# Sums of squares of the memory queries: squares as the weights of 32-column tiles with one column of ones, instead of ones as weights and a masked sum; and layer one's twelve transposes held four groups of matmuls longer

## The chip, the cores and the metric

One Trainium2 chip, one core of it. The metric is device microseconds (us) of one execution of the whole kernel, the median of three runs. The engines are named as the profile names them: PE is TensorE's matmuls, PEld its weight loads, DVE is VectorE, ACT is ScalarE, POOL is GpSimd, SP is SyncE, whose queue issues the loads of the weights.

## What is computed

Two layers of a hybrid decoder trunk over 256 tokens of width 1024. What matters here is one of three branches, attention of the tokens to a memory, with its query norm, and beside it the block-sparse attention whose probabilities are transposed (with 256 tokens its only block is the causal one).

```python
for l in range(2):
    h = rms_norm(x, norm_g[l])
    q_a, k_a, v_a, q_h, f_h, i_h, q_m, z = split(h @ w_in[l])          # eight groups of columns
    o_a = causal_attention(rope(rms_norm(q_a)), rope(rms_norm(k_a)), v_a)   # 8 heads x 64
    o_h = rms_norm(hgrn2(q_h, f_h, i_h))                               # 4 heads x 128
    qm  = rms_norm(q_m.reshape(B, S, 4, 128), mem_q_norm[l])           # a sum of 128 squares per token and head
    o_m = softmax(qm @ km.T / sqrt(128)) @ vm                          # km, vm from the 256 memory tokens
    x = x + (concat(o_a, o_h, o_m) * silu(z)) @ w_out[l]
```

## The kernel before

**Work and stages.** Every large product is made three times with float32 split into a high and a low part (`wh`, `wl` of the weights, `hT` or `yh`, `yl` of the other side), and added up in PSUM. The weights come in chunks of 128x1024: SP loads one into a buffer `wr`, ACT makes the high part of it (`h_to`, line 143), DVE the low part (`l_to`, line 158), PE uses both. There are four `wh` and three `wl` buffers, so ACT and DVE can be a few chunks ahead of PE and no more. A layer goes through its groups of columns in a fixed order, among them the query of the memory branch (`group_a` with `g_qm`, lines 263 and 1145) and right behind it the value of block-sparse attention (`group_b` with `g_va`, lines 204 and 729), and ends with the product with `w_out` (`w_out_phase`, line 1250; its matmuls are on line 1265). A `group_a` has four heads of one chunk each, every head eight groups of three matmuls of 256 columns (lines 272 to 274: `wh` twice, then `wl`). A `group_b` has four chunks of twelve matmuls of 512 columns (lines 213 to 216).

**What sets the order.** All else (norms, softmax, transposes) is written as generators that `step` (line 170) advances a piece at a time, at slots in the matmul loops; `yield n` waits n slots, `room` waits for one of four PSUM tiles named `sd`. Where the code doesn't pin instructions, the framework's scheduler orders them when the program is built. The order of each engine is then fixed: an instruction that waits holds all that stands behind it on its engine.

**Around the change.** `g_qm` is called with the accumulators of two heads at a time. ACT casts them to `qmh` (line 1153) and squares them into `sq` (line 1155): 128 partitions are the 128 numbers of a head, the columns are (head of the pair, half of the tokens t, group g of 32 tokens, token s). The sums over the partitions are wanted with tokens on the partitions. Before, eight matmuls a layer (line 1165, recorded at the helper's line 202 with tiles `sd` and `sq,ones`) take 32 columns of ones as weights and 128 columns of squares as the moving side; each puts into 32 partitions 32 equal rows. DVE then multiplies with a repeated identity `m32` (line 1168) and adds up (line 1170), which leaves each token its own sum in `ssq`; `rsq` (line 595) makes of it the inverse root, on DVE (line 597) and POOL. The scores of the memory branch (line 1193) don't need it; their softmax does (lines 1202 and 1208).

**The transposes.** `g_moba_unit(l, u)` (line 1040) is the softmax of half of the eight block-sparse heads: exponentials on ACT (line 1086), their sums' reciprocal `ria` on DVE (line 1091), eight multiplications of `P` by it on DVE (line 1095: four of 128x128 for the first half of the tokens, then four of 128x256), and twelve transposes on PE (line 1108) in three blocks of four, each block into one `sd` tile that ACT copies out (line 1109). For u = 1 the first block needs only the first four multiplications. For u = 0 in layer one, line 1099 holds the transposes until head 2 of the memory query is done, and line 1107 has the scheduler put them behind the matmul `T["last"]`. PSUM tiles that they may wait for are those of `y_transpose` (line 777; PE line 781, ACT line 784, DVE line 785).

Of the kernel before, what the change touches and what calls it, by code (L numbers as in the profile page):

```python
# [12 lines left out]
F32 = mybir.dt.float32  # L13
# [5 lines left out]
OP = mybir.AluOpType  # L19
AX = mybir.AxisListType  # L20
# [26 lines left out]
def hymba_kernel(ctx: ExitStack, tc: tile.TileContext, front, x, x_t, mem, mem_t, positions, w_in, w_out, w_mem_kv,  # L47
                 moba_g, out):
    nc = tc.nc
    cst = ctx.enter_context(tc.tile_pool(name="cst", bufs=1))  # L50
    sb = ctx.enter_context(tc.tile_pool(name="sb", bufs=1))
# [6 lines left out]
    def acc_tile():  # L58
        return psum.tile([128, 512], F32, name="acc", tag="acc", bufs=4)
# [4 lines left out]
    def room(what, n=1):  # L64
        while held[what] + n > room_of[what]:
            yield

    def take(*whats):
        for w in whats:
            yield from room(w)  # L70
        while any(held[w] >= room_of[w] for w in whats):
            yield
        for w in whats:
            held[w] += 1

    def side_tile():
        held["sd"] += 1
        assert held["sd"] <= 4
        return psum.tile([128, 512], F32, name="sd", tag="sd", bufs=4)

    def rel(what="sd", n=1):
        held[what] -= n

    def small(name, n):
        return sb.tile([128, n], F32, name=name, tag=name, bufs=2)
# [39 lines left out]
    def dma_to(n):  # L125
        while st["dma"] < min(n, len(chunks)):
            i = st["dma"]
            ap = chunks[i][1]
            raws[i] = sb.tile([128, 1024], F32, name="wr", tag="wr", bufs=RAW_BUFS)
            load(raws[i], ap)  # L130
            st["dma"] += 1
# [4 lines left out]
    def h_to(n):  # L136
        while st["h"] < min(n, len(chunks)):
            i = st["h"]
            off = 16 if chunks[i][0] == "A" else 0
            whs[i] = sb.tile([128, 1088], F32R, name="wh", tag="wh", bufs=WH_BUFS)[:, off:off + 1024]  # L140
            g = chunks[i][2]
            if g is None:
                ins = nc.scalar.copy(whs[i], raws[i])  # L143
                if i == 12:
                    pin(ins)
            else:
                for sl in parts(i):
                    nc.scalar.activation(whs[i][:, sl], raws[i][:, sl], AF.Copy, scale=gT[:, g:g + 1])  # L148
            st["h"] += 1

    def l_to(n):
        while st["l"] < min(n, len(chunks)):
            i = st["l"]
            off = 16 if chunks[i][0] == "A" else 0
            wls[i] = sb.tile([128, 1088], F32R, name="wl", tag="wl", bufs=WL_BUFS)[:, off:off + 1024]
            g = chunks[i][2]
            if g is None:
                nc.vector.tensor_tensor(wls[i], raws[i], whs[i].bitcast(F32), op=OP.subtract)  # L158
            else:
                for sl in parts(i):  # L160
                    nc.vector.scalar_tensor_tensor(wls[i][:, sl], in0=raws[i][:, sl], scalar=gT[:, g:g + 1],  # L161
                                                   in1=whs[i][:, sl].bitcast(F32),
                                                   op0=OP.mult, op1=OP.subtract)
            st["l"] += 1

    active = []
    done = set()
    T = {}

    def step():  # L170
        for e in list(active):
            e[0] -= 1
            if e[0] <= 0:
                try:
                    e[0] = next(e[1]) or 1
                except StopIteration:
                    active.remove(e)

    def spawn(gen, delay=1):
        active.append([delay, gen])  # L180
# [8 lines left out]
    def slot(first):  # L189
        if first:  # L190
            c = st["c"]
            dma_to(c + 1 + DMA_AHEAD)
            h_to(c + 1 + H_AHEAD)
            l_to(c + 1 + L_AHEAD)
        step()

    def mm(o, a, b, s, e):
        nc.tensor.matmul(o, lhsT=a, rhs=b, start=s, stop=e)  # L198


    def mm_row(o, a, b):
        tc.keep_in_program_order(nc.tensor.matmul(o, lhsT=a, rhs=b, start=True, stop=True))  # L202
# [60 lines left out]
    def group_a(thl, each, name=None):  # L263

        for h in range(4):
            i = st["c"]
            if h % 2 == 0:
                acc = acc_tile()
            o = acc[:, (h % 2) * 256:(h % 2) * 256 + 256]
            for k in range(8):  # L270
                wH, wL = whs[i][:, k * 128:(k + 1) * 128], wls[i][:, k * 128:(k + 1) * 128]
                mm(o, wH, thl[:, k, 0], k == 0, False)
                mm(o, wH, thl[:, k, 1], False, False)
                last = nc.tensor.matmul(o, lhsT=wL, rhs=thl[:, k, 0], start=False, stop=k == 7)  # L274
                if k == 3:
                    slot(False)
            T["last"] = last.ins
            done.add((name, h))
            st["c"] += 1
            del whs[i], wls[i], raws[i]  # L280
            if h % 2:
                spawn(each(h - 1, acc))
            slot(True)
# [45 lines left out]
    pt = side_tile()  # L329
# [3 lines left out]
    ident = cst.tile([128, 128], F32, name="ident")  # L333
# [253 lines left out]
    def heads(t, n):  # L587
        return t.rearrange("p (h d) -> p h d", h=n)
# [6 lines left out]
    def rsq(name, ss, n, width):  # L595
        ms = small(name + "m", n)
        nc.vector.tensor_scalar(ms, ss, 1.0 / width, EPS, op0=OP.mult, op1=OP.add)
        r = small(name + "r", n)
        nc.gpsimd.tensor_tensor(r, ms, pw[:, :n], op=OP.pow)
        return r  # L600
# [55 lines left out]
        T["vm"] = vmh, vml  # L656
        yield

    m32 = cst.tile([128, 32], F32, name="m32")
    ones32 = cst.tile([128, 32], F32, name="ones32")  # L660

    def g_m32():
        nc.vector.memset(ones32, 1.0)
        nc.vector.tensor_reduce(m32, ident.rearrange("p (g s) -> p s g", g=4), AX.X, OP.add)
        yield

    lbs = cst.tile([128, 2, 4], F32, name="lbs")

# [371 lines left out]
    def g_moba_unit(l, u):  # L1040
# [10 lines left out]
        for t in range(2):  # L1051
# [18 lines left out]
            for i in range(4):  # L1070
                c = t * 4 + i
# [11 lines left out]
        for t in range(2):  # L1083
            for i in range(4):
                c, r = t * 4 + i, t * 8 + 2 * i + u
# [6 lines left out]
        for t in range(2):  # L1092
            for i in range(4):
                c = t * 4 + i
                nc.vector.tensor_scalar(P[:, i, kc[t]], P[:, i, kc[t]], ri[:, c:c + 1], None, op0=OP.mult)  # L1095
        yield 2
        tag = ("PTh", "PTl")[u]
        yield from take(tag)
        while u == l == 0 and ("qm0", 2) not in done:
            yield  # L1100
        PT = sb.tile([128, 4, 384], F32, name="PT", tag=tag, bufs=1)
        for b in (1, 2, 0) if u == 0 and l == 1 else range(3):
            bs = slice(b * 128, (b + 1) * 128)
            yield from room("sd")
            pt = side_tile()
# [17 lines left out]
        for w in range(2):  # L1123
            for i in range(4):
                p, e = 2 * w + i // 2, i % 2
                h = 2 * p + e
                rows, c = slice(64 * e, 64 * e + 64), (i // 2) * 256
# [17 lines left out]
    def g_qm(l, h0, acc):  # L1145
        if h0 == 0:
            T["qm"] = (sb.tile([128, 4, 256], F32R, name="qmh", tag="ih", bufs=1),
                       sb.tile([128, 1088], F32R, name="qml", tag="hF", bufs=1)[:, 16:1040].rearrange(
                           "p (k s) -> p k s", k=4))
            T["q2"] = []  # L1150
        qmh, qml = T["qm"]
        hs, a = slice(h0, h0 + 2), heads(acc, 2)
        nc.scalar.copy(qmh[:, hs], a)
        sq = sb.tile([128, 512], F32, name="sq", tag="sq", bufs=2)
        nc.scalar.activation(sq, acc, AF.Square)
        T["q2"].append(sq.rearrange("p (h t g s) -> p h t g s", h=2, t=2, g=4))
        nc.vector.tensor_tensor(qml[:, hs], a, qmh[:, hs].bitcast(F32), op=OP.subtract)
        if h0 == 0:
            return
        yield 2  # L1160
        yield from room("sd")
        pt = side_tile()
        for u, sq in reversed(list(enumerate(T.pop("q2")))):
            for g in range(4):
                mm_row(pt[g * 32:g * 32 + 32, u * 128:u * 128 + 128], ones32, sq[:, :, :, g])
        ss = small("ssq", 8)
        sd = sb.tile([128, 512], F32, name="sq", tag="sq", bufs=2)[:, :256]
        nc.vector.tensor_tensor(sd.rearrange("p (a s) -> p a s", s=32), pt[:, :256].rearrange("p (a s) -> p a s", s=32),
                                m32[:, None, :].to_broadcast([128, 8, 32]), op=OP.mult)
        nc.vector.tensor_reduce(ss.rearrange("p (t h) -> p h t", t=2), sd.rearrange("p (h t s) -> p h t s", t=2, s=32),  # L1170
                                AX.X, OP.add)
        rel()
        r = rsq("qm", ss, 8, 128)
        nr = small("nrm", 8)
        nc.gpsimd.tensor_scalar(nr, r, -1.0, None, op0=OP.mult)
        yield 2
        T.pop(f"y{M_}", None)
        for u in range(2):
            spawn(g_mem_unit(l, u, (qmh, qml), r, nr))
            yield 3  # L1180
# [154 lines left out]
    spawn(g_norm0(), 5)  # L1335
    spawn(g_mem_r(), 6)
    spawn(g_loads(), 5)
    spawn(g_m32(), 40)
    spawn(setup, 8)
    for l in range(DEPTH):  # L1340
        group_kv(mTh, mTl, lambda a: g_km(l, a), lambda a: g_vm(l, a), side_tile)
# [73 lines left out]
```

## Time and profile before

| what | us |
|---|---|
| three runs | 394.71, 394.89, 395.28 |
| median | 394.89 |
| the profiled execution, its own time | 394.93 |
| its span in the trace | 393.1 |
| PE busy | 388.5 |
| weight loads (PEld) busy | 355.2 |
| DVE busy | 314.5 |
| ACT busy | 254.4 |
| POOL busy | 68.2 |

The times are of the whole execution; the span runs from the first to the last instruction of the trace, 1.8 us less. In rows of the timeline the columns are the start in us from the span's beginning, the duration in us of all instructions of the row together, the engine, the line, the operation, what it writes and reads, its shape, how often, and in brackets how long the engine stood idle ahead of it and for whom. A matmul's recorded duration reaches into the next one's: the next starts before the last has ended, so the pace is read from the starts. A float32 matmul of the program is two records on PE; one whose operands are the split parts is one.

### The profile page before, as it was taken

The page shows a single profiled execution, that of the slowest core. Times are in us where ns is not written, and L with a number is a line of the kernel's source. Part 1 is how long each engine was busy: PE and PEld are TensorE (multiplying, and loading weights), DVE is VectorE, ACT ScalarE, POOL GpSimd, SP SyncE. Part 2 cuts the span into 40 slices and gives each one's busy share as a digit, 9 for nine tenths or more (in the row PEclk, how much of TensorE's full clock was granted, in tenths as well). Part 3 has the DMA queues.
Part 4 walks back from the last instruction along what each step waited for, and adds up shares of the span by engine and source line. Part 5 has one row for each costly group of instructions (what it writes and reads, how often), then busy time and mean ns, then how long its engine had stood idle before and what let it go on. Part 6 is the DMA issues. An engine that isn't in the chain of part 4 may idle for free.

```text
span 393.1 us, 8138 instructions
## 1 busy us (share of the span) xinstructions
PE 388.5 (99%) x3166; PEld 355.2 (90%) x3166; DVE 314.5 (80%) x634; ACT 254.4 (65%) x407; POOL 68.2 (17%) x94
## 2 busy tenths in 40 slices
PE   8999999999999999999999999999999999999996
PEld 6889988888999988999988999888889999799996
DVE  5799989999993859776586999799999695578653
ACT  6788876438837999644463786445685974958420
POOL 2006824540001002000061030033400200010000
PEclk9999999999999999999999999999999999999999
DMA  7998564459553364433546375636664265444203
GB/s 270 418 354 287 190 228 143 163 154 262 184 206 108 108 215 160 155 115 108 207 168 214 111 237 191 212 108 216 200 207 155 84 198 190 154 155 162 84 25 108
DMA packets 22663, 70.95 MB, mean 180 GB/s; under 512 B 2528, under 2 KB 5984, under 8 KB 22624
## 3 DMA queue, kind: packets, MB, share of 16 engines
q1 hardware_dynamic: 19872, 67.86, 51.2%
q10 hardware_dynamic: 2752, 2.56, 2.4%
q8 instruction: 25, 0.41, 0.4%
q14 instruction: 14, 0.11, 0.1%
HBM read 67.27 MB, written 1.05 MB: 174 GB/s over the span
## 4 chain that ended last, share of the span: by engine, by line
PE 96%; DMA 1%; DVE 1%; ACT 0%; SPq 0%; issue 0%; DVEq 0%
PE acc L198 51%; PE acc L1265 17%; PE sd L198 11%; PE acc L274 9%; PE sd L202 2%; PE sd L1129 1%; DMA mw<-in_front_dram 1%; PE sd L1108 1%; PE sd L1020 1%; PE sd L1227 1%; PE sd L637 0%; DVE P L1095 0%; PE sd L781 0%; SPq L123 0%; DVE yl L785 0%
## 5 line engine op out<-in xcount | busy, mean ns | idle before, releaser
L143 ACT CAST wh<-wr 128x1024 fp32r<-128x1024 f32 x104 | 108.7, 1051 | 73.6 <-PE acc L198 40.9
L158 DVE TENSOR_TENSOR wl<-wr,wh 128x1024 fp32r<-128x1024 f32 x104 | 126.5, 1220 | 22.0 <-PE acc L1265 5.1
L198 PE MATMUL acc<-hT,wh 128*128 128x256 f32 x640 | 111.9, 278 | 0.0
L198 PE MATMUL acc<-wh,hT 128*128 128x512 f32 (+1 forms) x322 | 100.8, 390 | 0.0
L198 PEld LDWEIGHTS acc<-hT,wh 128*128 128x128 f32 x640 | 96.8, 188 | 0.1
L274 PE MATMUL acc<-hT,wl 128*128 128x256 f32 x320 | 88.2, 277 | 0.0
L198 PEld LDWEIGHTS acc<-wh,hT 128*128 128x128 f32 x322 | 60.4, 188 | 12.6 <-issue 0.2
L198 PE MATMUL acc<-wl,hT 128*128 128x512 f32 x160 | 63.0, 394 | 0.0
L274 PEld LDWEIGHTS acc<-hT,wl 128*128 128x128 f32 x320 | 59.9, 188 | 0.1
L1265 PE MATMUL acc<-yh,wl 128*128 128x256 f32 x128 | 35.6, 279 | 0.0
L198 PEld LDWEIGHTS acc<-wl,hT 128*128 128x128 f32 x160 | 30.0, 188 | 6.0 <-DVE ria L1091 0.2
L1265 PE MATMUL acc<-yl,wh 128*128 128x256 f32 x128 | 35.4, 277 | 0.0
L1265 PE MATMUL acc<-yh,wh 128*128 128x256 f32 x128 | 34.9, 278 | 0.0
L1265 PEld LDWEIGHTS acc<-yl,wh 128*128 128x128 f32 x128 | 24.0, 188 | 0.1
L1265 PEld LDWEIGHTS acc<-yh,wl 128*128 128x128 f32 x128 | 24.0, 188 | 0.0
L1265 PEld LDWEIGHTS acc<-yh,wh 128*128 128x128 f32 x128 | 23.8, 188 | 0.1
L161 DVE SCALAR_TENSOR_TENSOR wl<-wr,gT,wh 128x1024 fp32r<-128x1024 f32 (+1 forms) x14 | 19.0, 1374 | 4.7 <-PE acc L198 2.0
L148 ACT ACTIVATE wh<-wr,gT 128x1024 fp32r<-128x1024 f32 (+1 forms) x14 | 15.1, 1090 | 10.4 <-DMA wr<-in_w_mem_kv_dram 3.5
L1265 PE MATMUL acc<-y,wh 128*128 128x256 f32 x128 | 21.8, 276 | 0.0
L1265 PEld LDWEIGHTS acc<-y,wh 128*128 128x128 f32 x128 | 19.2, 188 | 0.0
L1265 PE MATMUL acc<-y,wl 128*128 128x256 f32 x64 | 17.5, 276 | 0.0
L1086 ACT ACTIVATE P<-P,nba,rq 128x128 f32<-128x128 f32 (+1 forms) x32 | 17.2, 538 | 0.1
(253 smaller groups left out, 669.0 us busy)
## 6 DMA issues: line engine op xcount, KB each, us to landing
wr<-in_w_in_dram SPq DMA_DIRECT2D x80, 512.0 KB, 3.7
wr<-in_w_out_dram SPq DMA_DIRECT2D x24, 512.0 KB, 3.6
wr<-in_w_mem_kv_dram SPq DMA_DIRECT2D x12, 512.0 KB, 3.5
k<-k ACTq DMA_DIRECT2D x8, 256.0 KB, 5.0
zT<-in_x_dram SPq DMA_DIRECT2D x2, 512.0 KB, 9.0
xs<-in_x_t_dram SPq DMA_DIRECT2D x2, 512.0 KB, 9.8
memr<-in_mem_dram SPq DMA_DIRECT2D x2, 512.0 KB, 6.7
mw<-in_front_dram SPq DMA_DIRECT2D x2, 384.0 KB, 5.3
```

The costliest lines, as they stand in the source:

```text
L143: ins = nc.scalar.copy(whs[i], raws[i])
L148: nc.scalar.activation(whs[i][:, sl], raws[i][:, sl], AF.Copy, scale=gT[:, g:g + 1])
L158: nc.vector.tensor_tensor(wls[i], raws[i], whs[i].bitcast(F32), op=OP.subtract)
L161: nc.vector.scalar_tensor_tensor(wls[i][:, sl], in0=raws[i][:, sl], scalar=gT[:, g:g + 1], in1=whs[i][:, sl].bitcast(F32), op0=OP.mult, op ...
L198: nc.tensor.matmul(o, lhsT=a, rhs=b, start=s, stop=e)
L202: tc.keep_in_program_order(nc.tensor.matmul(o, lhsT=a, rhs=b, start=True, stop=True))
L274: last = nc.tensor.matmul(o, lhsT=wL, rhs=thl[:, k, 0], start=False, stop=k == 7)
L1020: nc.tensor.transpose(pt[:, p * 128:(p + 1) * 128], kr[:, t, p * 128:(p + 1) * 128], ident)
L1086: pin(nc.scalar.activation(P[:, i, kc[t]], P[:, i, kc[t]], AF.Exp, bias=nb[:, c:c + 1], scale=rq[:, r:r + 1], accum_out=sm[:, c:c + 1]))
L1108: pin(nc.tensor.transpose(pt[:, i * 128:(i + 1) * 128], P[:, i, bs], ident))
L1129: pin(nc.tensor.matmul(po[w][rows, c + o:c + 256], lhsT=va[:, b, h * 64:(h + 1) * 64], rhs=PT[e][:, p, 256 * b:256 + 128 * b], start=b == ...
L1265: ins = nc.tensor.matmul(a, lhsT=wt, rhs=y, start=first and (to is not None or b % 2 == 0), stop=n == nk - 1 and j == 2, skip_group_check= ...
```

## The change

Three things change, and with them what the scheduler makes of the order.

- The sums of squares. A tile of 32 columns of squares is now the weights, and one column of ones (`ones1`) the moving side. Each matmul leaves the sums of 32 tokens in 32 partitions of one column; for 256 tokens and four heads that are 32 matmuls a layer, into eight columns of a PSUM tile. The masked multiplication and the reduction on DVE go, and `rsq` reads the eight columns from PSUM.
- `ones32` and `m32`, which were made at the start (lines 659 to 665), go; `ones1` is set there.
- `group_a` marks a head as done, and sets `T["last"]`, after the fourth of a head's eight groups instead of after the eighth. Line 1099 waits for head 3 instead of head 2. So the twelve transposes of u = 0 in layer one move from the end of head 2 to the middle of head 3.

```diff
@@ group_a @@
                 if k == 3:
+                    T["last"] = last.ins
+                    done.add((name, h))
                     slot(False)
-            T["last"] = last.ins
-            done.add((name, h))
@@ constants @@
-    m32 = cst.tile([128, 32], F32, name="m32")
-    ones32 = cst.tile([128, 32], F32, name="ones32")
-
-    def g_m32():
-        nc.vector.memset(ones32, 1.0)
-        nc.vector.tensor_reduce(m32, ident.rearrange("p (g s) -> p s g", g=4), AX.X, OP.add)
-        yield
+    ones1 = cst.tile([128, 64], F32, name="ones1")[:, 0:1]
+    nc.vector.memset(ones1, 1.0)
@@ g_moba_unit @@
-        while u == l == 0 and ("qm0", 2) not in done:
+        while u == l == 0 and ("qm0", 3) not in done:
             yield
@@ g_qm @@
         for u, sq in reversed(list(enumerate(T.pop("q2")))):
-            for g in range(4):
-                mm_row(pt[g * 32:g * 32 + 32, u * 128:u * 128 + 128], ones32, sq[:, :, :, g])
-        ss = small("ssq", 8)
-        sd = sb.tile([128, 512], F32, name="sq", tag="sq", bufs=2)[:, :256]
-        nc.vector.tensor_tensor(sd.rearrange("p (a s) -> p a s", s=32), pt[:, :256].rearrange("p (a s) -> p a s", s=32),
-                                m32[:, None, :].to_broadcast([128, 8, 32]), op=OP.mult)
-        nc.vector.tensor_reduce(ss.rearrange("p (t h) -> p h t", t=2), sd.rearrange("p (h t s) -> p h t s", t=2, s=32),
-                                AX.X, OP.add)
+            for c in range(4):
+                i = c % 2 * 4 + 2 * u + c // 2
+                for g in range(4):
+                    mm_row(pt[g * 32:g * 32 + 32, i:i + 1], sq[:, c // 2, c % 2, g], ones1)
+        r = rsq("qm", pt[:, 0:8], 8, 128)
         rel()
-        r = rsq("qm", ss, 8, 128)
```

What the scheduler now puts where is seen in the order of the instructions, at three places on PE. The program after is nine or ten lines shorter, so that line 1108 (the transposes of `P`) is 1103 in it, and 1265 is 1256.

The first place is layer one, the memory query's heads 2 and 3 (`acc<-hT,wh` and `acc<-hT,wl` are its matmuls, a head ends after eight groups of three). Before:

```order
L198 MATMUL acc<-hT,wh 128x256 x2
L274 MATMUL acc<-hT,wl 128x256
L1108 MATMUL sd<-ident,P 128x128 x12
L198 MATMUL acc<-hT,wh 128x256 x2
L274 MATMUL acc<-hT,wl 128x256
L198 MATMUL acc<-hT,wh 128x256 x2
L274 MATMUL acc<-hT,wl 128x256
L198 MATMUL acc<-hT,wh 128x256 x2
L274 MATMUL acc<-hT,wl 128x256
L198 MATMUL acc<-hT,wh 128x256 x2
L274 MATMUL acc<-hT,wl 128x256
```

Now, from the same place on:

```order
L198 MATMUL acc<-hT,wh 128x256 x2
L274 MATMUL acc<-hT,wl 128x256
L198 MATMUL acc<-hT,wh 128x256 x2
L274 MATMUL acc<-hT,wl 128x256
L198 MATMUL acc<-hT,wh 128x256 x2
L274 MATMUL acc<-hT,wl 128x256
L198 MATMUL acc<-hT,wh 128x256 x2
L274 MATMUL acc<-hT,wl 128x256
L198 MATMUL acc<-hT,wh 128x256 x2
L274 MATMUL acc<-hT,wl 128x256
L1103 MATMUL sd<-ident,P 128x128 x12
```

The twelve transposes stood between head 2 and head 3; now four groups of head 3 stand ahead of them.

The second place is layer one, the third chunk of `g_va` (`acc<-wh,hT` and `acc<-wl,hT` are its matmuls), with the sums of squares (`sq` and the ones) and the first block of u = 1's transposes. Before:

```order
L198 MATMUL acc<-wh,hT 128x512
L202 MATMUL sd<-sq,ones_177 32x128 x8
L198 MATMUL acc<-wh,hT 128x512
L198 MATMUL acc<-wl,hT 128x512
L198 MATMUL acc<-wh,hT 128x512 x2
L198 MATMUL acc<-wl,hT 128x512
...
L1265 MATMUL acc<-yh_1796,wh 128x256
L1265 MATMUL acc<-yl_1797,wh 128x256
L1108 MATMUL sd<-ident,P 128x128 x4
```

Now:

```order
L198 MATMUL acc<-wl,hT 128x512
L198 MATMUL acc<-wh,hT 128x512 x2
L202 MATMUL sd<-ones_176,sq 32x1 x32
L1103 MATMUL sd<-ident,P 128x128 x4
L198 MATMUL acc<-wl,hT 128x512
L198 MATMUL acc<-wh,hT 128x512 x2
```

The sums stand four matmuls later, and the four transposes, which stood behind the rest of `g_va` and the first two matmuls of `w_out`, follow right behind them.

The third place is the same stage of layer two. Before:

```order
L198 MATMUL acc<-wh,hT 128x512 x2
L202 MATMUL sd<-sq,ones_177 32x128 x8
L198 MATMUL acc<-wl,hT 128x512
L198 MATMUL acc<-wh,hT 128x512 x2
L198 MATMUL acc<-wl,hT 128x512
...
L1265 MATMUL acc<-yl_4019,wh 128x256
L1108 MATMUL sd<-ident,P 128x128 x4
```

Now:

```order
L198 MATMUL acc<-wh,hT 128x512 x2
L202 MATMUL sd<-ones_176,sq 32x1 x32
L1103 MATMUL sd<-ident,P 128x128 x4
L198 MATMUL acc<-wl,hT 128x512
L198 MATMUL acc<-wh,hT 128x512 x2
```

Here the sums stand where they stood, and the four transposes have come to stand right behind them as well. On DVE the multiplications of `P` (line 1095) stay behind the same instructions as before: the same three `wl` and the same `qml` in layer one, in another order. On ACT one `wh` cast of layer one stands two exponentials earlier; all that stands ahead of the last exponential is the same.

More of the change, by code (lines that the diff above doesn't have):

```diff
@@ L1337, in hymba_kernel @@
     spawn(g_loads(), 5)
-    spawn(g_m32(), 40)
     spawn(setup, 8)
```

## Prediction

> **What bounds the kernel now.** I read the page's busy times first, then its chain, then the waits of PE.
>
> ```profile
> PE 388.5 (99%) x3166; PEld 355.2 (90%) x3166; DVE 314.5 (80%) x634; ACT 254.4 (65%) x407; POOL 68.2 (17%) x94
> ...
> PE 96%; DMA 1%; DVE 1%; ACT 0%; SPq 0%; issue 0%; DVEq 0%
> ```
>
> PE is busy for 388.5 of the 393.1 us of the span, and 96% of the chain that ended last is PE. DVE and ACT count only where PE waits for them, and the list of waits of PE has three rows:
>
> ```profile
> PE sd L198 <- PEq L1404: 0.8, 1, 0.8
> PE sd L198 <- ACT wh L148: 0.5, 2, 0.3
> PE sd L1108 <- DVE yl L785: 0.4, 1, 0.4
> ```
>
> Two are at the start. The third lies where the change moves the twelve transposes. So time can be won in two ways, by less work on PE or by that wait, and it can be lost wherever an instruction is moved on PE to a place where its operand isn't ready yet. I take the three moves in turn, each from PE's, DVE's and ACT's timelines around it.
>
> **The twelve transposes of layer one.** PE and DVE there:
>
> ```profile
> 137.00 0.28 PE L274 MATMUL acc<-hT,wl 128*128 128x256 f32 x1
> 137.12 1.04 PE L1108 MATMUL sd<-ident,P 128*128 128x128 f32 x8
> 138.51 0.66 PE L1108 MATMUL sd<-ident,P 128*128 128x128 f32 x4 [0.36 <-DVE yl L785]
> 138.93 0.48 PE L198 MATMUL acc<-hT,wh 128*128 128x256 f32 x2
> ...
> 140.42 0.40 PE L198 MATMUL acc<-hT,wh 128*128 128x256 f32 x2
> ...
> 136.58 1.22 DVE L158 TENSOR_TENSOR wl<-wr,wh 128x1024 fp32r<-128x1024 f32 x1
> 137.71 0.75 DVE L785 SCALAR_TENSOR_TENSOR yl<-sd,gT,yh 128x512 fp32r<-128x512 f32 x1
> ...
> 316.71 1.48 PE L1108 MATMUL sd<-ident,P 128*128 128x128 f32 x12
> 318.02 0.60 PE L781 MATMUL sd<-ident,zh 128*128 128x128 f32 x4
> ```
>
> The third block of four waits for a PSUM tile until DVE's `yl` ends at 137.71 + 0.75 = 138.46; PE goes on at 138.51, 0.05 us later, which I take as the handoff everywhere. From 137.12 to 138.93 the twelve cost 1.81 us; undisturbed in layer two they cost 318.02 - 316.71 = 1.31. The wait is worth 0.50 us.
>
> Held four groups longer, they find the tile free. But the groups that now stand ahead are head 3's, whose first `wl` is the one that DVE makes from 136.58 to 137.80. Head 3 begins at 137.12 instead of 138.93, its first `wl` matmul is the third, due at about 137.35, and waits until 137.85: again 0.50 us. Then the other ten matmuls of the four groups at a pace of about 0.115 us and the transposes at 1.31: 137.85 + 1.15 + 1.31 = 140.31. Before, the same work was done at 140.42. So this part is worth 0.1 us, and what hides it comes next; DVE works without a gap from the multiplications of `P` through this `wl` to `yl`, so nothing brings it earlier.
>
> **The sums and the four transposes of layer one.** Before:
>
> ```profile
> 148.44 0.39 PE L198 MATMUL acc<-wh,hT 128*128 128x512 f32 x1
> 148.75 0.64 PE L202 MATMUL sd<-sq,ones 128*32 128x128 f32 x16
> 149.33 0.50 PE L198 MATMUL acc<-wh,hT 128*128 128x512 f32 x1
> 149.67 0.40 PE L198 MATMUL acc<-wl,hT 128*128 128x512 f32 x1
> 149.91 0.63 PE L198 MATMUL acc<-wh,hT 128*128 128x512 f32 x2
> 150.38 0.40 PE L198 MATMUL acc<-wl,hT 128*128 128x512 f32 x1
> ...
> 153.82 0.60 PE L1108 MATMUL sd<-ident,P 128*128 128x128 f32 x4
> ```
>
> The sums take PE from 148.44 + 0.23 (the pace of a 512-column matmul, 149.91 - 149.67 = 0.24) = 148.67 to 149.33: 0.66 us. In the new order four matmuls of 0.23 come first, so the sums can begin at 148.67 + 0.92 = 149.59, and the transposes follow at once. Those need the first four multiplications of `P`, which come out of this chain:
>
> ```profile
> 150.54 0.19 ACT L1086 ACTIVATION_READ_ACCUMULATOR P<-P,nba,rq 128x1 f32 x1
> ...
> 150.76 0.20 DVE L1091 RECIPROCAL ria<-sma 128x8 f32<-128x8 f32 x1
> 151.00 1.93 DVE L1095 TENSOR_SCALAR P<-P,ria 128x128 f32<-128x128 f32 x8
> ...
> 151.20 0.68 DVE L1095 TENSOR_SCALAR P<-P,ria 128x128 f32<-128x128 f32 x3
> ...
> 142.21 1.28 ACT L1086 ACT_TABLE_LOAD   x1
> 143.51 0.49 ACT L1086 ACTIVATE P<-P,nba,rq 128x128 f32<-128x128 f32 x1
> ```
>
> The last exponential's sum is read until 150.73, the reciprocal starts at 150.76, and the row from 151.20 (the second to the fourth multiplication) ends at 151.88. ACT is at work without a gap from the table load at 142.21 to that point, and the change only swaps instructions ahead of it; so the fourth multiplication stays at 151.88 and the transposes start at 151.93. Before, they stood at 153.82, 1.9 us behind it, and nobody waited.
>
> Now PE stands still until 151.93. By then it has done what it had done at 150.38 before (the sums and the four matmuls): **+1.55 us**. The price of the new sums, and the 0.1 us from above, don't enter: both fall into the wait, as long as the sums need less than 151.93 - 149.59 = 2.34 us. Behind the transposes the rest of `g_va` follows; DVE and ACT have their `wl` and `wh` ready by then, and the scores, softmax and products of the memory branch move with PE, so the wait is not won back.
>
> **The same in layer two.**
>
> ```profile
> 341.79 0.61 PE L198 MATMUL acc<-wh,hT 128*128 128x512 f32 x2
> 342.33 0.64 PE L202 MATMUL sd<-sq,ones 128*32 128x128 f32 x16
> 342.91 0.50 PE L198 MATMUL acc<-wl,hT 128*128 128x512 f32 x1
> ...
> 342.88 1.93 DVE L1095 TENSOR_SCALAR P<-P,ria 128x128 f32<-128x128 f32 x8
> ...
> 343.08 0.68 DVE L1095 TENSOR_SCALAR P<-P,ria 128x128 f32<-128x128 f32 x3
> ...
> 333.96 1.06 ACT L143 CAST wh<-wr 128x1024 fp32r<-128x1024 f32 x1 [1.66 <-PE acc L198]
> ```
>
> The sums begin where they began, at 341.79 + 0.46 = 342.25. The fourth multiplication ends at 343.08 + 0.68 = 343.76, so the transposes start at 343.81, and PE is then where it was at 342.91: **+0.90 us**. That ACT's chain doesn't run ahead while PE is late in layer one is seen in the cast at 333.96: it waited 1.66 us for PE to free a buffer, and the exponentials follow from it without a gap. PE and that chain move together.
>
> **The price of the sums.** It matters in layer two if they need more than 343.81 - 342.25 = 1.56 us. They are 64 records a layer instead of 16. Nearest are 32-column tiles with 32 moving columns; far off is the one case of a single moving column, with weights of the full width:
>
> ```profile
> 97.59 0.35 PEld L202 LDWEIGHTS sd<-hKQ 128*32 128x32 f32 x32 [0.36 <-issue]
> 97.98 0.55 PEld L202 LDWEIGHTS sd<-hQ,hK 128*64 128x64 f32 x16
> ...
> 207.45 0.50 PE L463 MATMUL sd<-ones,xc 128*128 128x1 f32 x4
> 207.81 0.48 PE L198 MATMUL acc<-wh,mTh 128*128 128x512 f32 x1
> ```
>
> The first 32 records take 97.98 - 97.59 = 0.39 us, 12 ns each: 64 make 0.78, and with at most the 0.36 us for which the weight loads stood still at that change of tiles (the first row's bracket) 1.14. The four on line 463 take 0.36, 90 ns each: 64 make 5.8. I take 12 ns, which is of the same tiles; the low end is the 0.66 of now or less, and changes nothing. Up to (1.56 - 0.36) / 64 = 19 ns each the sum stands. On DVE two instructions a layer go:
>
> ```profile
> 152.84 0.42 DVE L1168 TENSOR_TENSOR sq<-sd,m 128x256 f32<-128x256 f32 x1
> ...
> 154.31 0.41 DVE L1170 TENSOR_REDUCE ssq<-sq 128x8 f32<-128x256 f32 x1
> ```
>
> They stand behind the multiplications of `P`, so they don't bring those earlier, and what follows from them, the softmax of the memory branch, has PE's matmuls of `w_out` beside it. They and the reduction at the start are worth nothing.
>
> On this the Trainium skill has a rule that speaks against the change. "TensorE: Matmul & The Clock Gate", under "Wait — 56ns, not 53.3ns?", says that the start-to-start time of matmuls stays at 25 ns or more however few columns move, and "TensorEngine Tiling (Array Packing)", under "Instruction Overhead", that one moving column costs as much as 60. By that, an estimate, 64 records take 1.6 us. The rows above go below it: with four column tiles in turn, records stand 12 ns apart.
>
> **The sum.** 394.93 + 1.55 + 0.90 = 397.38 for the profiled execution's own time; the median of the runs is 0.04 below that, so 397.34, rounded to 397.3.
>
> **The rivals.**
> - *Only layer one's wait is there* (in layer two the chain of ACT and DVE comes early against a PE that is late). For it: the wait there is the smaller one. Against it: the cast at 333.96. 394.89 + 1.55, and the dearer sums of layer two at 0 to 1.14 - 0.66 = 0.48: 396.4 to 396.9. Chance 0.12.
> - *The small matmuls hold PE one by one.* At 25 ns, twice the row's pace, and with the 0.36 they take 1.96 us: layer one still hides it, layer two ends them at 342.25 + 1.96 = 344.21, 0.40 later than above: 397.7; chance 0.04. (This is what the rule of the Trainium skill's page "TensorE: Matmul & The Clock Gate" would make of this kernel.) At the 90 ns of line 463, 5.8 us: 149.59 + 5.8 instead of 150.38 and 342.25 + 5.8 instead of 342.91 make +5.0 and +5.1: 405.0. Against it stand the rows of 32 columns. Chance 0.02.
> - *The chain comes early in both layers*, so that both waits together are under 0.79 us: 394.9 to 395.7. The multiplications would have to end 0.8 us earlier in each. But the reciprocal follows the last exponential's sum by 0.03 us (150.73 and 150.76), and the exponentials are ACT's work without a gap. Chance 0.08.
> - *Faster: the hold pays, and P is ready.* If the fourth multiplication ended by 149.4 in layer one and 342.6 in layer two, and `wl` by 137.3, the 0.50 us would be won, and sums at 0.4 us would win 0.26 in each layer: 394.89 - 1.02 = 393.9. It decides at those three times; the trace has 151.88, 343.76 and 137.80. Chance 0.04.
>
> **How the numbers follow.** My own case keeps 0.70: 397.3. 0.2% of the time is 0.79 us, about what a measurement of this kernel tells from no change. Slower by more than that: 0.70 + 0.12 + 0.06 = 0.88; within it 0.08; faster 0.04. The range reaches down to the first rival with 0.2 to spare, 396.2. It reaches up by one cast of ACT (1.06 us, the row at 333.96), should the cast that moved ahead of two exponentials have to wait there and delay the multiplications: 397.34 + 1.06 = 398.4. That holds 0.70 + 0.12 + 0.04 = 0.86, less some of their tails.
>
> **What would show it.** In the list of waits of PE two new rows: line 1103's transposes waiting for DVE's `P`, about 1.2 us in layer one and 0.4 in layer two by my price of the sums, at about 152 and, moved by 1.55, 345 us. The row of `yl` is gone, and an `acc` matmul waits about 0.5 us for `wl` at 137.4. The sums' 64 records take 0.8 to 1.1 us. The forecast is wrong if the transposes follow the sums without a wait, and its step on the hold if no `wl` wait stands at 137.4.

## The result and the profile after

The changed kernel took 398.59 us (median of 6 runs, 397.18 to 399.46), the kernel before 395.35 beside it (6 runs, 394.71 to 395.55): a ratio of 1.0082, 95% interval 1.0066 to 1.0097. It is slower, as forecast, and 0.19 us above the top of the forecast's range. The six runs fall into two groups: at a granted clock of 1.0 (the share of its full speed that PE's clock had, as a mean over the run) they took 397.18, 397.34 and 398.24 us; at a mean clock of 0.996 they took 398.93, 399.08 and 399.46. The profiled one is the 397.34 (span 395.5, clock 1.0), for which the sum of the prediction said 397.38.

The busy times on its page, and its list of waits of PE (engine, tile and line, what was waited for: us in total, times, the longest):

```profile
PE 389.0 (98%) x3262; PEld 355.6 (90%) x3262; DVE 313.2 (79%) x629; ACT 255.2 (65%) x407; POOL 68.7 (17%) x94
```

```profile
PE sd L1103 <- DVE P L1090: 2.4, 2, 1.6
PE sd L198 <- PEq L1394: 0.8, 1, 0.8
...
PE acc L274 <- DVE wl L158: 0.3, 1, 0.3
```

The first row is new: the transposes wait twice for DVE's `P`, 2.4 us in all. The row of `yl` is gone, and one of `wl` has come. PE's timeline at the twelve transposes, then at the sums of layer one and of layer two:

```profile
137.84 0.38 PE L274 MATMUL acc<-hT,wl 128*128 128x256 f32 x1 [0.34 <-DVE wl L158]
139.12 1.47 PE L1103 MATMUL sd<-ident,P 128*128 128x128 f32 x12
140.35 0.48 PE L198 MATMUL acc<-hT,wh 128*128 128x256 f32 x2
...
149.68 0.71 PE L202 MATMUL sd<-ones,sq 128*32 128x1 f32 x64
152.00 0.63 PE L1103 MATMUL sd<-ident,P 128*128 128x128 f32 x4 [1.61 <-DVE P L1090]
...
343.97 0.71 PE L202 MATMUL sd<-ones,sq 128*32 128x1 f32 x64
345.44 0.66 PE L1103 MATMUL sd<-ident,P 128*128 128x128 f32 x4 [0.76 <-DVE P L1090]
```

And DVE's in the same two places, the reciprocal and the multiplications on which the transposes wait:

```profile
150.74 0.20 DVE L1086 RECIPROCAL ria<-sma 128x8 f32<-128x8 f32 x1
150.98 1.92 DVE L1090 TENSOR_SCALAR P<-P,ria 128x128 f32<-128x128 f32 x8
...
344.51 1.93 DVE L1090 TENSOR_SCALAR P<-P,ria 128x128 f32<-128x128 f32 x8
```

The reader should see two things. DVE's chain did not move in layer one (reciprocal at 150.74, before 150.76) and moved by 1.63 us in layer two (344.51, before 342.88), which is just what PE had lost by then. And PE's transposes now start 152.00 - 150.38 = 1.62 us behind the point that PE had reached at 150.38 before, and 345.44 - 342.91 = 2.53 us behind it in layer two. So this profile follows the prediction to 0.1 us. What is missing from the forecast is in the other half of the runs.

### The profile page after: what moved, and what is told of

It is laid out like the page before. It is cut to its first block, busy times and chain, and to the rows that moved or that the text cites. A ratio compares the mean times of both kernels' runs of the same rounds, so it can differ in the third digit from the quotient of the medians.

```text
span 395.5 us, 8327 instructions
## 1 busy us (share of the span) xinstructions
PE 389.0 (98%) x3262; PEld 355.6 (90%) x3262; DVE 313.2 (79%) x629; ACT 255.2 (65%) x407; POOL 68.7 (17%) x94
## 4 chain that ended last, share of the span: by engine, by line
PE 61%; DVE 0%; issue 0%; DVEq 0%
PE acc L198 27%; PE acc L1256 17%; PE sd L198 7%; PE acc L274 5%; PE sd L1124 1%; PE sd L1103 1%; PE sd L202 1%; PE sd L1218 1%; PE sd L1015 0%; DVE P L1090 0%; PE sd L637 0%; PE sd L776 0%; PE sd L463 0%; DVE xs L1291 0%; PE sd L426 0%
```

## The experiments

The theory with which they began: the two waits cost what they are long (1.55 and 0.90 us), and in some runs the first of them, in which PE stands still, lets the granted clock of PE fall for a while; that is the 1.8 us of the second group. Rivals: the 64 one-column matmuls ahead of the wait bring the clock down; the late `P` or DVE's work does; the falls are chance and the kernel before has them too; the new sums cost time of their own.

**The changed kernel again.** No edit. First five, then six more runs:

> The changed kernel once more, to see how often its granted clock falls. Theory (waits and clock): the two waits of the transposes for P always cost 1.55 and 0.90 us, 397.2 to 398.2 us at a clock of 1.0, and in about half of the runs the clock is granted at 0.996 and the time is 1.8 us higher, 398.9 to 399.5; median 397.5 to 399. Rival (chance of the chip): the clock falls in as many runs of the kernel before.

> The changed kernel a third time, for more runs and, with luck, a profile of one in which the clock falls. Theory (the stand of PE in layer one lets the clock fall in some runs): 397.2 to 398.3 us at clock 1.0, and some runs at about 0.996 and 398.9 to 399.5; in a profile of such a run the clock is at half speed for one stretch of about 3.4 us that begins while PE stands at 150.3 to 152. Rival (the falls of the first six runs were chance): none here, nor in the kernel before.

The first gave 397.43 us (397.3 to 397.89, 5 runs; ratio 1.0059, 1.0046 to 1.0071), all at clock 1.0: none of the falls that were expected in about half of the runs, and a median just under the expected 397.5. The second gave 397.78 us (397.06 to 399.3, 6 runs; ratio 1.0073, 1.0053 to 1.0092), two of them at 0.996 with 399.18 and 399.3. The kernel before, in every run beside these, was at 0.999 or 1.0. None of the profiled runs so far had a fall in it, so four single profiled runs followed:

> One more profile of the changed kernel. If the clock falls in it, at about 0.996 and 398.9 to 399.5 us: by the theory (PE's stand in layer one) at half speed for one stretch of about 3.4 us that begins between 151 and 154 us; by the rival (something else) anywhere else. If it does not fall: 397.0 to 398.2 us at 1.0.

> The same look again: a fall, if there is one, begins between 151 and 154 us by the theory, anywhere else by the rival.

> The same look again: a fall, if there is one, begins between 151 and 154 us by the theory, anywhere else by the rival.

> The same look again: a fall, if there is one, begins between 151 and 154 us by the theory, anywhere else by the rival.

They took 397.30 and 397.73 us at clock 1.0, and 398.76 and 399.21 at 0.996. The third of these runs has a fall. Its windows of 1 us (length; busy time of PE, PEld, DVE, ACT, POOL with the instructions in each; then PE's granted clock, the DMA share and GB/s):

```profile
150.00:151.00 1.00, 0.15 (x18) 0.07 (x7) 0.96 (x3) 1.00 (x3) 0.00 (x0) 1.00 0.00 0
151.00:152.00 1.00, 0.17 (x1) 0.20 (x2) 1.00 (x6) 0.47 (x1) 0.00 (x0) 0.91 0.20 53
152.00:153.00 1.00, 1.00 (x5) 1.00 (x5) 0.80 (x4) 0.05 (x1) 0.12 (x1) 0.50 0.95 373
153.00:154.00 1.00, 1.00 (x4) 0.71 (x4) 0.56 (x1) 0.73 (x2) 1.00 (x1) 0.50 0.25 98
154.00:155.00 1.00, 1.00 (x4) 0.81 (x3) 0.66 (x1) 0.85 (x1) 0.76 (x2) 0.50 0.07 16
155.00:156.00 1.00, 1.00 (x6) 0.80 (x5) 0.00 (x0) 0.00 (x0) 0.00 (x0) 0.89 0.44 74
```

Windows of 0.2 us around both ends of it:

```profile
151.80:152.00 0.20, 0.17 (x1) 0.20 (x2) 0.20 (x2) 0.00 (x0) 0.00 (x0) 0.54 0.42 102
155.00:155.20 0.20, 0.20 (x2) 0.18 (x1) 0.00 (x0) 0.00 (x0) 0.00 (x0) 0.50 0.00 0
155.20:155.40 0.20, 0.20 (x2) 0.14 (x1) 0.00 (x0) 0.00 (x0) 0.00 (x0) 0.93 0.00 0
```

And PE's timeline of the same run:

```profile
151.83 1.09 PE L1103 MATMUL sd<-ident,P 128*128 128x128 f32 x4 [1.67 <-DVE P L1090]
152.56 0.78 PE L198 MATMUL acc<-wl,hT 128*128 128x512 f32 x1
153.14 1.05 PE L198 MATMUL acc<-wh,hT 128*128 128x512 f32 x2
153.99 0.63 PE L198 MATMUL acc<-wl,hT 128*128 128x512 f32 x1
...
155.49 0.62 PE L198 MATMUL acc<-wh,hT 128*128 128x512 f32 x2
155.94 0.39 PE L198 MATMUL acc<-wl,hT 128*128 128x512 f32 x1
```

A mean of 0.54 over 151.80 to 152.00 says that the clock went from 1.0 to 0.5 at 151.82; 0.93 over 155.20 to 155.40 that it came back at 155.23. That is 3.41 us at half speed, and it begins as PE's wait of 1.67 us ends. PE works all through it, two 512-column matmuls taking 153.99 - 153.14 = 0.85 us where they take 155.94 - 155.49 = 0.45 after it, so the fall costs 3.41 / 2 = 1.7 us. The fourth run has the same with other times:

```profile
153.40:153.60 0.20, 0.20 (x2) 0.18 (x1) 0.20 (x1) 0.20 (x2) 0.20 (x1) 0.50 0.99 410
156.60:156.80 0.20, 0.20 (x2) 0.13 (x1) 0.00 (x0) 0.00 (x0) 0.00 (x0) 0.50 0.91 348
156.80:157.00 0.20, 0.20 (x2) 0.17 (x1) 0.00 (x0) 0.00 (x0) 0.00 (x0) 0.97 0.66 266
```

There PE waited until 152.25, and the clock fell at 153.40 and came back at 156.81: again 3.41 us. Both falls began between 151 and 154 us, as the theory said. Over all 21 runs of the changed kernel the clock fell in 7; the median of the 14 others is 397.41 us, that of the 7 is 399.18, and the difference of 1.77 is the 1.7 of the profile.

**The four transposes later.** In these three, the transposes of `u = 1` are issued only when `g_va` is half-way through its last chunk, which puts them eight `g_va` matmuls behind the sums, and the memory branch waits for them. The hold of the transposes stands in both layers, in layer one alone, and in layer two alone:

```
                 if (c, j) == (3, 0):
+                    done.add(name)                # name is b0, b1 for g_va
...
+        while u and f"b{l}" not in done:          # "and l == 0", "and l == 1"
+            yield
         PT = sb.tile([128, 4, 384], F32, name="PT", tag=tag, bufs=1)
...
+            done.add(("t", u, l))                 # behind each block of transposes
...
+        while ("t", 1, l) not in done:            # in g_qm, ahead of the memory branch
+            yield
```

> The four transposes of the second head of each pair stand eight g_va matmuls (1.84 us) later in both layers; the one-column sums and the hold stay. Theory (waits and clock): P is ready when PE gets there, no wait for P is left, 395.0 to 395.6 us, the clock 1.0 in all runs. Rival (the 64 one-column matmuls themselves bring the clock down, not the wait): the clock is 0.996 in about half of the runs, which then take 396.8 to 397.3. Rival (the sums themselves cost): 396 or more at a clock of 1.0.

> The transposes moved later in layer one only; layer two's wait stays. Theory (waits and clock): 0.90 us above the kernel before, 396.0 to 396.5 us, and the clock 1.0 in all runs, since layer two's wait of about 0.8 us is too short for the clock. Rival (layer two's wait, or the small matmuls, bring the clock down): 0.996 in about half of the runs, up to 398.

> The transposes moved later in layer two only; layer one's wait stays. Theory (waits and clock): 1.55 us above the kernel before, 396.7 to 397.2 us, in the runs at clock 1.0, and in about half of them the clock is 0.996 and the time 1.8 us higher, about 398.6. Rival (the clock has another cause than layer one's wait): no fall of the clock here, or as many in the run with the transposes later in layer one.

They took 397.45 us (396.57 to 397.6, 5 runs; ratio 1.0048, 1.0035 to 1.0062), 396.69 (396.56 to 397.29; 1.0042, 1.0029 to 1.0054) and 398.23 (398.1 to 398.95; 1.0080, 1.0067 to 1.0092). The clock fell in one run of the third (398.95, 0.996), in none of the others. The waits for `P` went where they should. The list of waits of the first:

```profile
PE sd L198 <- ACT wh L148: 1.0, 1, 1.0
PE sd L198 <- PEq L1401: 0.8, 1, 0.8
PE acc L198 <- ACT wh L148: 0.5, 1, 0.5
PE acc L276 <- DVE wl L158: 0.4, 1, 0.4
```

(The waits for `wh` on line 148 stand at 5 to 7 us, at the first loads, and differ from run to run.) No wait for `P`, and yet only a part of the loss is back: all three medians lie above what was expected, by 1.9, 0.2 and 1.0 us over the top of each range. In the profiled runs it is in the pace of `w_out`. Every third matmul of one stretch in the first of these kernels:

```profile
188.47 0.28 PE L1263 MATMUL acc<-y,wl 128*128 128x256 f32 x1
...
190.24 0.28 PE L1263 MATMUL acc<-y,wl 128*128 128x256 f32 x1
```

Six rows of this kind, 15 matmuls apart: (190.24 - 188.47) / 15 = 118 ns. In the kernel before:

```profile
188.27 0.28 PE L1265 MATMUL acc<-y,wl 128*128 128x256 f32 x1
...
190.31 0.28 PE L1265 MATMUL acc<-y,wl 128*128 128x256 f32 x1
```

Seven rows, 18 matmuls apart: 113 ns, at the same granted clock of 1.00. From the end of the 64-column products (behind which `w_out` goes on) to the first matmul of the next layer, the first of these kernels takes 199.54 - 169.44 = 30.10 us and the kernel before 197.90 - 168.78 = 29.12 with the same matmuls in it: 0.98 us more. In the second kernel, the profiled run (397.29) is one of two at about 397.3; the other three took 396.56 to 396.69, so the slower pace may not come in full in every run. In these kernels `w_out` follows those products; before, and in the changed kernel, eight transposes do. So a fourth kernel moved the transposes without holding the memory branch back, which leaves the eight transposes where they were:

```
+        while u and f"b{l}" not in done:
+            yield
         PT = sb.tile([128, 4, 384], F32, name="PT", tag=tag, bufs=1)
```

> The four transposes again eight g_va matmuls later in both layers, but the memory branch is not held back with them: its first twelve score matmuls follow the sums, and the transposes of L1222 stand right behind the 64-column products, as in the kernel before. Theory (waits, and the pace of the w_out matmuls): no wait for P, and the 256-column matmuls of w_out keep their 0.113 us behind those products instead of the 0.118 of the two kernels with the transposes moved alone; 395.2 to 395.7 us. Rival (what stayed in those kernels is the price of the sums, or of the hold, and not of the pace): 396.4 us or more, as there.

It took 395.54 us (394.94 to 396.01, 11 runs; ratio 1.0006, 0.9997 to 1.0014), with no wait for `P` and no fall of the clock. The same rows in it:

```profile
188.04 0.28 PE L1260 MATMUL acc<-y,wl 128*128 128x256 f32 x1
...
190.08 0.28 PE L1260 MATMUL acc<-y,wl 128*128 128x256 f32 x1
```

18 matmuls in 2.04 us, 113 ns. The sums and the first matmul behind them, with no wait between:

```profile
150.05 0.71 PE L202 MATMUL sd<-ones,sq 128*32 128x1 f32 x64
150.69 0.38 PE L198 MATMUL sd<-kml,qmh 128*128 128x256 f32 x1
```

With the sums and the hold of the changed kernel in it and only the waits taken out, the loss is gone (the interval is -0.12 to 0.55 us); so the new sums and the hold cost nothing that these runs can tell, and the waits, with the falls of the clock, are all of it.

**Each part alone.** The new sums without the hold (the two lines of `group_a` and the `while` as before), and the hold without the new sums (these lines alone):

```
                 if k == 3:
+                    T["last"] = last.ins
+                    done.add((name, h))
                     slot(False)
-            T["last"] = last.ins
-            done.add((name, h))
...
-        while u == l == 0 and ("qm0", 2) not in done:
+        while u == l == 0 and ("qm0", 3) not in done:
```

> The new sums without the hold. In layer one the four transposes stand sixteen g_va matmuls behind the sums, in layer two right behind them as in the changed kernel. Theory (each wait costs what it is long, and both parts of the change together make layer one's): no wait for P in layer one, 0.8 us of it in layer two, 0.90 us in all: 396.0 to 396.6 us, clock 1.0 in all runs. Rival (the 64 records cost by themselves): 397 or more, or a clock of 0.996 in some runs.

> The hold of the twelve transposes without the new sums. Theory (the wait for yl is replaced by one for wl, and both are worth the same): 395.1 to 395.6 us, no wait for P, one of 0.3 to 0.5 us for wl near 137.5. Rival (the hold brings PE forward): 394.9 or less. Rival (the hold makes layer one's wait by itself): 396.9 or more.

The sums alone: 395.93 us (395.64 to 396.47, 11 runs; ratio 1.0023, 1.0014 to 1.0032), just under the expected range. The interval, 0.55 to 1.26 us, holds the 0.90 of layer two. Its list of waits has one wait for `P` where the changed kernel has two, and `yl` is back:

```profile
PE sd L1103 <- DVE P L1090: 0.8, 1, 0.8
PE sd L198 <- PEq L1394: 0.8, 1, 0.8
PE sd L1103 <- DVE yl L780: 0.4, 1, 0.4
```

The hold alone: 395.37 us (394.89 to 395.96, 11 runs; ratio 1.0006, 0.9997 to 1.0015), as expected, with a wait of 0.3 us for `wl` in place of the one for `yl`. So neither part makes layer one's wait; the two together do: with the hold, four more `g_va` matmuls stand ahead of the sums, and only with both parts do the transposes stand right behind them. The clock fell in none of these 22 runs.

**The wait made longer, and filled.** In the next two, PE's order is pinned from layer one's transposes on, so that they stand four `g_va` matmuls further ahead; in the second of them DVE also passes twice over `P` before its multiplications:

```
+        for _ in range(2 if u > l else 0):        # the second kernel only
+            nc.vector.tensor_scalar(P[:, :, 0:256], P[:, :, 0:256], 1.0, None, op0=OP.mult)
         nc.vector.reciprocal(ri, sm)
...
+            if (u, l, b) == (1, 0, 0):
+                T["pin"] = True                   # mm and part pin what they issue while it is set
```

> Between the changed kernel and the one with the longest wait: PE's order is pinned, so that the transposes of layer one stand four g_va matmuls (0.92 us) further ahead, but DVE does no more than in the changed kernel. Theory (the longer PE stands, the surer the clock falls): a wait of 2.5 us and more in layer one; the clock falls in more runs than in the changed kernel and in fewer than, or as many as, in the one with the longest wait; 398.0 to 398.8 us at clock 1.0, 399.8 to 401 with a fall. Rival (only the extra work of DVE brings the clock down): no fall.

> The wait of layer one made longer: in layer one the multiplication of P's second head is preceded by two passes of DVE over 1024 columns of it (times one, about 2.3 us), and PE's order is pinned, so that the transposes stand four g_va matmuls further ahead and PE can't pass them. Theory (a long stand of PE lets the clock fall): a wait for P of 4 to 5.5 us, and the clock at 0.996 or less in most of the runs: 400 to 401.5 us where it stays at 1.0, 402 to 403.5 where it falls. Rival (the falls have nothing to do with the wait): clock 1.0 in all runs or in as many as before, 400 to 401.5.

The first took 401.13 us (401.01 to 401.22, 4 runs; ratio 1.0150, 1.0137 to 1.0163) with clocks of 0.994 to 0.996, the second 402.31 (402.06 to 403.29, 4 runs; 1.0189, 1.0175 to 1.0203) with 0.991 to 0.996. The clock fell in all eight runs. The first is 0.1 us above the range expected with a fall; the second is in its range, though its wait is shorter than the 4 to 5.5 us expected, since DVE's two passes took 0.7 us each and not 2.3 together. The waits of layer one, first of the one, then of the other:

```profile
152.49 0.63 PE L1105 MATMUL sd<-ident,P 128*128 128x128 f32 x4 [2.58 <-DVE P L1092]
```

```profile
153.63 2.99 PE L1107 MATMUL sd<-ident,P 128*128 128x128 f32 x12 [3.81 <-DVE P L1094]
```

The windows of the second kernel around that wait:

```profile
150.00:151.00 1.00, 0.00 (x0) 0.00 (x0) 1.00 (x1) 1.00 (x4) 0.00 (x0) 1.00 0.00 0
151.00:152.00 1.00, 0.00 (x0) 0.00 (x0) 1.00 (x4) 1.00 (x3) 0.00 (x0) 0.66 0.00 0
152.00:153.00 1.00, 0.00 (x0) 0.00 (x0) 1.00 (x4) 0.05 (x1) 0.27 (x1) 0.50 0.78 201
...
157.00:158.00 1.00, 1.00 (x7) 1.00 (x6) 0.06 (x1) 0.24 (x1) 0.00 (x0) 0.50 0.00 0
158.00:159.00 1.00, 1.00 (x8) 0.96 (x8) 0.81 (x2) 0.00 (x0) 0.00 (x0) 0.93 0.00 0
```

0.66 over 151 to 152 puts the fall at 151.32, and 0.93 over 158 to 159 the return at 158.14: 6.82 us, twice 3.41. PE had stood for only 153.63 - 3.81 = 149.82 to 151.32, 1.5 us, when the clock fell. The last two are this kernel with the old sums (the mask and the reduction with them), and this kernel with PE at work in the wait, by matmuls of a constant behind the sums:

```
+        one = nc.const_aps.tensor(1.0, [128, 256], BF)
+        for _ in range((32, 6)[l]):
+            mm_row(pt[:, 256:512], one[:, :128], one)
         r = rsq("qm", pt[:, 0:8], 8, 128)
```

> The kernel with the longest wait with the old sums (128 columns of ones, the mask and the reduction) instead of the one-column sums; the hold stays. Theory (PE's standing still, not the one-column matmuls, lets the clock fall): the clock falls in most runs here too, 0.991 to 0.996, and layer one costs what it costs with the new sums. Rival (the clock falls because of the 64 one-column matmuls ahead of the wait): 1.0 in all runs.

> The kernel with the longest wait, but behind the sums PE makes 32 matmuls (layer one) and 6 (layer two) of a constant into columns that nobody reads, so that it works while it would stand. Theory (PE's standing still is what lets the clock fall): the transposes wait no longer than the constant's matmuls take to the arrival of P at the same time as there, the clock is 1.0 in all runs, and the time is 399.3 to 400.3 us, some 2 to 3 below the kernel with the longest wait. Rival (late P, DVE's extra work or the one-column matmuls bring the clock down): 0.991 to 0.996 as there, 402 or more.

With the old sums: 402.95 us (401.64 to 403.05, 4 runs; ratio 1.0189, 1.0172 to 1.0205), the clock at 0.991 to 0.996 in all four. The one-column matmuls are not needed for the fall. In its profiled run the clock was at half from 154.23 to 157.64, in that of the first pinned kernel from 152.98 to 156.40 (by the same working from windows of 0.2 us: 0.58 over 154.20 to 154.40 and 0.89 over 157.60 to 157.80; 0.96 over 152.80 to 153.00 and 0.51 over 156.20 to 156.40): 3.41 and 3.42 us. Filled: 400.77 us (400.6 to 401.14, 4 runs; ratio 1.0145, 1.0130 to 1.0159), the clock at 0.999 to 1.0 in all four, 1.5 us below the kernel that it fills. PE's timeline in it:

```profile
149.43 3.76 PE L204 MATMUL sd<-const-bfloat16-1.0 128*128 128x256 bf16 x32
153.29 0.63 PE L1107 MATMUL sd<-ident,P 128*128 128x128 f32 x4
```

The transposes start 4.51 us behind the start of the sums (148.78); unfilled they started 153.63 - 149.11 = 4.52 behind it. The work on PE goes on at the same time, DVE's extra work and the one-column matmuls are there, and only the standing still is gone, and with it the fall. Its time lies 0.5 us above what was expected of it; its `w_out` matmuls stood 118 ns apart ahead of the 64-column products (71 of them from 162.20 to 170.56), as those of the two pinned kernels did.

All runs together, by how long PE stood at the transposes of layer one:

| PE stands | kernels | runs with a fall |
|---|---|---|
| not at all | transposes later (both layers, layer one, scores first), sums alone, hold alone | 0 of 43 |
| 1.6 to 1.7 us | the changed kernel; transposes later in layer two | 8 of 26 |
| 2.6 us | pinned | 4 of 4 |
| 3.8 to 4.3 us | pinned with DVE's passes, new sums and old | 8 of 8 |
| the same, filled | PE at work on a constant | 0 of 4 |

Layer two's wait of 0.76 us alone stands in 16 of the 43 (sums alone, and transposes later in layer one).

## Why the prediction was right, and where it failed

- **The hold, 0.1 us: right by the trace.** `wl` took the place of `yl`: the matmul due at about 137.34 started at 137.84, 0.50 us late, as forecast (the bracket's 0.34 counts only from the recorded end of the matmul ahead), and PE went on behind the twelve at 140.35 (forecast 140.31, before 140.42). The runs can't tell so little from nothing: alone it measured 1.0006 (0.9997 to 1.0015).
- **Layer one, +1.55 us: right in place, cause and size.** The transposes started at 152.00 (forecast 151.93), released by DVE's `P`, and PE had lost 1.62 us.
- **Layer two, +0.90 us: right.** 2.53 - 1.62 = 0.91, and the sums alone, which have only this wait, cost 0.55 to 1.26. The rival in which only layer one waits is out.
- **The price of the sums: right that it falls into the waits, a little high.** Where no wait follows, the next matmul starts 0.64 us behind the sums' start (150.05 and 150.69 in the kernel with the scores first), 10 ns for each of the 64 records; before, 16 records took 0.58. The forecast had 0.8 to 1.1. So the waits look longer than forecast (1.61 and 0.76 instead of about 1.2 and 0.4) and cost the same. The rivals of 25 and of 90 ns a record are out; the rule of the Trainium skill's "TensorE: Matmul & The Clock Gate" that matmuls start 25 ns apart or more does not hold for these records in four column tiles.
- **Nothing is won back: right.** The scores, the softmax and `w_out` moved with PE: from the end of the 64-column products to the next layer it is 29.12 us before and after.
- **The step that failed is the sum.** 394.93 + 1.55 + 0.90 = 397.38 met the profiled run (397.34) and the runs without a fall (median 397.41). But it added the waits to a span in which PE's clock stays at 1.0: a fall of the clock was put at nothing, without a reason, in the sum, in the rivals and in the range, whose top was taken from one cast of ACT (1.06 us). A PE that stands for 1.6 us is not only late: in 7 of 21 runs its clock then fell to half for 3.41 us, worth another 1.77 us. In the six runs behind 398.59 it fell in three, and their median lies between the two groups. How many runs fall is chance: in the five and the six runs that followed it fell in none and in two, and their medians, 397.43 and 397.78, lie inside the range. That is luck, since the sum lacks the term all the same. A term "1.7 us in some runs" would have put the top of the range at 399.1.

The Trainium skill has the mechanism on a page that the prediction used for another rule: "TensorE: Matmul & The Clock Gate", Part 1, says that the clock is halved after an idle window of 3.41 us that runs free of the program. The length agrees with the five falls measured here (3.41, 3.41, 3.41, 3.42 and 6.82 us). Under "Why this matters for your kernels" it asks for no idle gaps over about 3 us; here gaps of 2.6 us were enough in 4 runs of 4 and gaps of 1.6 to 1.7 in 8 of 26, so as a bound on what is safe it is too wide. That a gap of 1.6 us brings a fall only in some runs would follow if most of the gap has to lie inside one of those windows. The traces with a fall fit that, if stretches of 3.41 us are counted back from it: the one that ends at the fall holds 1.50 us or more of standing in all five (1.50 in the kernel with the longest wait, 149.82 to 151.32), and the one before it, in the kernel with the old sums, holds 1.26 (149.56 to 150.82) and brought none. But if 1.50 us were enough and the windows lay at random, an estimate, a gap of 1.65 us would bring a fall in (3.41 + 1.65 - 2 x 1.50) / 3.41 = 60% of the runs, and it did in 8 of 26. No run here sets a window's phase, so how much of a gap decides stays open.

## What to carry to other kernels

When a wait on the busiest engine is to be priced, its length is the lower end; look also at whether that engine's clock stays where it is, since a stand of PE of 1.6 us among dense work cost another 1.7 us in a third of the runs, and one of 0.76 us cost nothing more in 16. When an edit replaces or moves some work, ask first what a scheduler puts right behind it: here the transposes moved up behind the new sums, ahead of the `P` that they need. And look at the single runs before the median: two groups 1.8 us apart, with another clock each, are two cases and not one with scatter.

## What the runs showed that was not expected

- The clock of PE fell 1.5 us after PE had stopped (149.82 to 151.32, in the kernel with the longest wait), and in the fourth single run 1.15 us after PE had gone back to work (152.25 to 153.40). Matmuls whose results nobody reads kept it up, in 4 runs of 4.
- The same 256-column matmuls, with the same operands in the same order and at a granted clock of 1.00, ran 113 ns apart in some kernels and 118 ns apart in others, for 10 to 30 us at a time, worth up to 1 us a layer. In the kernels with the transposes alone moved, the slower pace went with `w_out` following the 64-column products, and it was gone where transposes followed them; but the pinned kernels had it ahead of those products too (71 matmuls from 162.73 to 171.10 at 118 ns), with the transposes in that place. What sets it is open.
